# A decoder layer on one core: silu and two high-part copies of ScalarE put behind its next copy out of PSUM

## The chip, the cores and the metric

The kernel runs on one core of one Trainium2 chip. The metric is the device time of one execution in microseconds (us): 1008.36 us before the change, the median of 3 runs (1008.08 to 1009.29). In the profile the engines are called PE (TensorE, matmuls), PEld (TensorE's weight loads), DVE (VectorE), ACT (ScalarE), POOL (GpSimd) and SP (SyncE, which issues most DMAs). Each engine works through its own list of instructions in order; an instruction that must wait for another engine holds up all that stand behind it in its list.

## The reference

One hybrid decoder layer in float32, SEQ = 256 tokens, D_MODEL = 2048: attention heads and pooling mixers behind one input projection, an output projection into the residual, and then a gated MLP of width D_FF = 5632. The change touches the MLP alone:

```python
def conv_ffn(h, w_up, conv_w, conv_b, w_down):
    u = h @ w_up                                   # 2048 -> 2 * 5632
    u_pad = jnp.pad(u, ((0, 0), (CONV_WIDTH - 1, 0), (0, 0)))
    y = conv_b
    for i in range(CONV_WIDTH):                    # causal, 3 taps
        y = y + conv_w[i] * u_pad[:, i:i + S]
    gate, val = jnp.split(y, 2, axis=-1)
    return (jax.nn.silu(gate) * val) @ w_down
```

## The kernel before, in words

**Numbers in two parts.** A float32 matrix is split into a high part (rounded by a copy to the type fp32r) and a low part (the matrix less its high part). ACT makes the high part with an `activation` copy, DVE the low part with a subtraction. A product is then three matmuls: high by high, high by low, low by high. Weights arrive in chunks of 128 x 2048 elements, 1 MB each: SP loads a chunk into `raw` (`load`), ACT writes `wh` (`high`, L182), DVE writes `wl` (`low`, L188), and that frees `raw` for a later load. In the part of the program looked at here ACT makes `wh` three chunks ahead of PE, and DVE `wl` two chunks ahead.

**The MLP in three thirds.** The 5632 hidden features are taken in groups of 256, and the groups in three thirds of 8, 8 and 6. A third first computes all its groups ("up": for each group a gate block and then a value block, `ps_feat`, L276 and L278), then multiplies its result `hid` by `w_down` ("down": `ps_down`, L876). A block is four halves of 8 pairs of matmuls, and two chunks of weights. In the down stage of five, five and three groups of a third the product of 2 x 2 quarters is done in seven products in place of eight. Those need sums of quarters of the activations (`left_sums`) and of the weights; the latter DVE makes from loaded quarters during the up stage (`make`, L196 to L198), one per pair of blocks in most pairs, and SP stores them.

**What follows a block.** When PE has finished a block, `conv_in` brings it out of PSUM: ACT copies one half of the columns into a scratch tile `fs` (L545, "the copy" below), DVE adds the other half (L546, "the add") and writes `u`, scaled by row (L799). At the start of the next block ACT forms the three taps of the convolution, `y` and two `z` (L809 and L811, six instructions). One chunk later DVE sums them (`taps`, L817, two instructions). For a gate block ACT then applies silu in place (L827). For a value block DVE multiplies by the gate (L843, "the product"), ACT writes the high part of `hid` (L844), and one chunk later DVE writes the low part (L856) and, for the groups with seven products, the sums `ls` (L865 to L867), whose high part ACT writes to `sums` (L869) and whose low part DVE writes one chunk later (L870).

**What sets the order.** The program is written out by hand, one step per half block. A step first issues what falls due at the start of a chunk (`wh`, `wl`, `make`, then what `later` put on an agenda for this step), then what is in `deferred`, then the matmuls, and after a block's last half `conv_in`. Thus in ACT's list silu of a gate block stands ahead of the copy of the following value block, and the high part of `hid` ahead of the copy of the following gate block. The scratch tiles `fs` and `z` share a ring of two buffers (`scratch`), so the copy of a block takes the buffer of the first `z` of the block before it.

Of the kernel before, what the change touches and what calls it, by code (L numbers as in the profile page):

```python
# [23 lines left out]
F32 = mybir.dt.float32  # L24
F32R = mybir.dt.float32r
AF = mybir.ActivationFunctionType
OP = mybir.AluOpType
# [69 lines left out]
def layer(ctx: ExitStack, tc: tile.TileContext, xT, wts, mix, mix12, par, rel_d, ident_d, icnt_d, out):  # L97
    nc = tc.nc
# [32 lines left out]
    late, turn_of = {}, [0]  # L131
# [411 lines left out]
    def add_halves(dst, ps):  # L543

        nc.scalar.activation(dst, ps[:, :, S:], AF.Copy)  # L545
        nc.vector.tensor_tensor(dst, ps[:, :, :S], dst, op=OP.add)  # L546

    def pool_window(ps, g):

        s = early.tile([P, 2, S], F32, name="pst", tag=("sq", "hn")[g % 2], bufs=(1, 3)[g % 2])  # L550
        add_halves(s, ps)
        nc.vector.tensor_tensor(pa[0][:, :, PAD:], s, rrow[:, None, :].to_broadcast([P, 2, S]), op=OP.mult)
        st["win", g] = s
# [45 lines left out]


    steps, hooks, pre, deferred = [], [], {}, []
    hold, splits, now, agenda = set(), [], [0], {}
    where = []

    def later(n, f):
        agenda.setdefault(now[0] + n, []).append(f)
# [106 lines left out]
    def block(name, dt=F32):  # L713
        return late["pool"].tile([P, SPAD + 1024], dt, name=name, tag="sums", bufs=5)[:, SOFF:SOFF + 1024]

    def residual(ps, g):
        x2, s = x2_tiles(2 * g, 2 * g + 2), scratch("fs")
        add_halves(s, ps)
        nc.vector.tensor_tensor(x2, s, x2, op=OP.add)
        if g == 0:  # L720
            nc.scalar.activation(late["sq"], x2, AF.Square)
            return
        s = late["pool"].tile([P, 2, S], F32, name="xs", tag="y0")
        nc.scalar.activation(s, x2, AF.Square)
        nc.vector.tensor_tensor(late["sq"], late["sq"], s, op=OP.add)
# [44 lines left out]
    def stats2():  # L770
        late["rrow"] = keep.tile([P, S], F32, name="rrow2", tag="rrow")
        a, b = scratch("rs0"), scratch("rs1")
        t = a[:, 0, :]
        mean_sq(t.rearrange("p (j a) -> p a j", a=32), late["row"].rearrange("p (a j) -> p a j", j=8))
        rsqrt(late["rrow"], t, S, late["pool"], (a[:, 1, :], b[:, 0, :]))
# [19 lines left out]
    def conv_in(ps):  # L795

        s = scratch("fs")
        add_halves(s, ps)
        nc.vector.tensor_tensor(late["u"][:, :, 2:], s, late["rrow"][:, None, :].to_broadcast([P, 2, S]), op=OP.mult)  # L799

    def conv(f0_, which):

        u = late["u"]
        y = late["pool"].tile([P, 2, S], F32, name="y", tag=f"y{which}")
        z = [scratch("z") for _ in range(2)]
        for m in range(2):
            f = f0_ + m
            cw = [col(C_CW + i * 2 * NF + f) for i in range(3)]
            nc.scalar.activation(y[:, m, :], u[:, m, 2:], AF.Identity, scale=cw[2], bias=col(C_CB + f))  # L809
            for i in range(2):  # L810
                nc.scalar.activation(z[i][:, m, :], u[:, m, 1 - i:1 - i + S], AF.Copy, scale=cw[1 - i])  # L811
        return y, z

    def taps(y, z):

        for t in z:
            nc.vector.tensor_tensor(y, y, t, op=OP.add)  # L817
        return y

    def gate(ps, g):  # L820
        if g == 0:
            stats2()
        conv_in(ps)

        def rest(parts):
            y = taps(*parts)
            nc.scalar.activation(y, y, AF.Silu)  # L827
            late["gate"] = y

        def start():  # L830
            parts = conv(2 * g, 0)
            later(2, lambda: rest(parts))
        deferred.append(start)

    def value(ps, g, j, seven, end):
        conv_in(ps)

        def rest(parts):
            if j == 0:
                late["hid"] = keep.tile([P, KT, 2, S], F32R, name="hid", tag="c")  # L840
            y = taps(*parts)
            hid, ks = late["hid"], slice(2 * j, 2 * j + 2)
            nc.vector.tensor_tensor(y, y, late["gate"], op=OP.mult)  # L843
            nc.scalar.activation(hid[:, ks, 0, :], y, AF.Copy)  # L844
            later(2, lambda: rest2(y, hid, ks))

        def start():
            parts = conv(NF + 2 * g, 1)
            if end:
                rest(parts)  # L850
            else:
                later(2, lambda: rest(parts))
        deferred.append(start)

        def rest2(y, hid, ks):
            nc.vector.tensor_tensor(hid[:, ks, 1, :], y, hid[:, ks, 0, :].bitcast(F32), op=OP.subtract)  # L856
            if seven:
                late["S", j] = left_sums(y)

    def left_sums(y):  # L860

        y = y.rearrange("p a (b n) -> p (a b) n", n=P)
        a11, a21, a12 = (y[:, i, :] for i in range(3))
        s = late["pool"].tile([P, 2, S], F32, name="ls", tag="ls").rearrange("p a (b n) -> p (a b) n", n=P)
        nc.vector.tensor_tensor(s[:, :2, :], y[:, 0:4:3, :], y[:, 1:2, :].to_broadcast([P, 2, P]), op=OP.subtract)  # L865
        nc.vector.tensor_tensor(s[:, 2, :], s[:, 1, :], a11, op=OP.add)
        nc.vector.tensor_tensor(s[:, 3, :], a12, s[:, 2, :], op=OP.subtract)  # L867
        parts = block("sums", F32R).rearrange("p (a b n) -> p a b n", a=2, n=P)
        nc.scalar.activation(parts[:, 0], s, AF.Copy)  # L869
        later(2, lambda: nc.vector.tensor_tensor(parts[:, 1], s, parts[:, 0].bitcast(F32), op=OP.subtract))  # L870
        return parts

    def product(ps, left, right, first, last):
# [241 lines left out]
```

## Time and profile before

| | before |
|---|---|
| time, median of 3 runs | 1008.36 us |
| the profiled execution: time, span | 1010.49 us, 1008.7 us |
| busy share of the span: PE, PEld, DVE, ACT | 99%, 85%, 81%, 60% |
| mean granted TensorE clock | 0.995 |
| MLP's first third: up, down | 177.33 us, 85.88 us |
| second third: up, down | 177.36 us, 87.44 us |
| last third: up, down | 130.60 us, 61.20 us |

The stages are cut where the matmuls change from `ps_feat` to `ps_down` and back. A row of a timeline has the start, the duration, the engine, the line and operation with the tiles written and read, and in brackets how long the engine was idle before it and what ended that. A row of waits has who waited for what, the total in us, how often, and the longest. A matmul's duration is modelled and overlaps the next; from the start of one matmul to the start of the next is the time that it holds the engine.

### The profile page before, as it was taken

Reading aid. Unit: us, or ns where it says so; the run is one execution under the profiler, and the core shown is the slowest. Engines: PE = TensorE matmul, PEld = TensorE weight load, DVE = VectorE, ACT = ScalarE, POOL = GpSimd, SP = SyncE. Lnnn points to the kernel's source line nnn. Section 1 sums busy time; section 2 is a strip of 40 time slices with the busy share of each in tenths; the row PEclk is TensorE's granted clock in tenths of the full one; section 3 lists DMA queues with packets and bytes.
Section 4 is the critical chain, followed back from the end, with each engine's and each line's share of the span. In section 5 each row is a group of like instructions: output and inputs, shape, how many; then the busy total and the mean of one; then the engine's idle time right before and its main releaser. Section 6 shows DMA issues by size and latency. Waiting matters only on the chain.

```text
span 1008.7 us, 13494 instructions
## 1 busy us (share of the span) xinstructions
PE 993.8 (99%) x5276; PEld 854.3 (85%) x5276; DVE 818.8 (81%) x853; ACT 608.6 (60%) x719; POOL 74.6 (7%) x134
## 2 busy tenths in 40 slices
PE   9999999999999999998999999999989999999998
PEld 7888888888888888886888888888868888888886
DVE  6776859866678878888989788888888888888896
ACT  6654545555548566666655556666774756666742
POOL 0202232211103300000000000000000000000000
PEclk9999999999999999999999999999989999999999
DMA  9958785699977887677977889777777988866682
GB/s 352 319 210 271 259 258 196 210 327 368 321 204 245 305 329 280 250 275 255 395 264 306 312 312 378 293 273 274 262 275 278 373 303 316 316 252 255 223 317 101
DMA packets 48895, 285.34 MB, mean 283 GB/s; under 512 B 6696, under 2 KB 9128, under 8 KB 20352
## 3 DMA queue, kind: packets, MB, share of 16 engines
q1 hardware_dynamic: 41776, 264.17, 70.6%
q0 software_dynamic: 7056, 20.33, 7.6%
q8 instruction: 41, 0.67, 0.3%
q14 instruction: 22, 0.18, 0.1%
HBM read 253.14 MB, written 39.72 MB: 290 GB/s over the span
## 4 chain that ended last, share of the span: by engine, by line
PE 61%; DVE 19%; issue 7%; ACT 7%; DMA 5%; POOL 1%; SPq 0%; DVEq 0%; ACTq 0%; POOLq 0%
PE ps_feat L276 22%; PE ps_down L876 20%; PE ps_feat L278 11%; DVE wl L188 8%; PE ps_val L254 4%; DVE y L817 2%; DVE fs L546 2%; ACT z L811 2%; PE ps_tok L264 2%; ACT fs L545 1%; ACT wh L182 1%; ACT y L809 1%; DVE raw L196 1%; DVE u L799 1%; DMA qT<-q1d 1%
## 5 line engine op out<-in xcount | busy, mean ns | idle before, releaser
L276 PE MATMUL ps_feat<-x2h,wh 128*128 128x512 f32 x1406 | 480.6, 390 | 0.0
L188 DVE TENSOR_TENSOR wl<-raw,wh 128x2048 fp32r<-128x2048 f32 (+1 forms) x171 | 376.0, 2204 | 25.2 <-PE ps_down L876 8.6
L278 PE MATMUL ps_feat<-x2h,wl 128*128 128x256 f32 x1408 | 390.2, 277 | 2.1 <-DVE wl L188 1.7
L182 ACT ACTIVATE wh<-raw 128x2048 fp32r<-128x2048 f32 (+1 forms) x171 | 316.0, 1852 | 101.2 <-PE ps_down L876 66.4
L276 PEld LDWEIGHTS ps_feat<-x2h,wh 128*128 128x128 f32 x1406 | 263.8, 188 | 55.6
L278 PEld LDWEIGHTS ps_feat<-x2h,wl 128*128 128x128 f32 x1408 | 264.2, 188 | 5.1 <-DVE wl L188 5.0
L876 PE MATMUL ps_down<-wh,hid 128*128 128x512 f32 x444 | 143.2, 391 | 0.0
L160 DVE TENSOR_TENSOR wl<-raw,wh 128x2048 fp32r<-128x2048 f32 (+3 forms) x44 | 83.0, 1894 | 37.7 <-ACT wh L159 29.2
L546 DVE TENSOR_TENSOR fs<-ps_feat,fs 128x512 f32<-128x512 f32 x52 | 36.0, 692 | 83.8 <-ACT fs L545 83.8
L876 PEld LDWEIGHTS ps_down<-wh,hid 128*128 128x128 f32 x444 | 84.1, 189 | 17.6
L876 PE MATMUL ps_down<-wl,hid 128*128 128x512 f32 x222 | 87.3, 393 | 0.8 <-DVE wl L188 0.8
L276 PE MATMUL ps_feat<-cat,wh 128*128 128x512 f32 x256 | 87.3, 389 | 0.0
L264 PE MATMUL ps_tok<-wh,xh 128*128 128x512 f32 x256 | 80.0, 391 | 0.0
L811 ACT ACTIVATE z<-u,pv 128x256 f32<-128x256 f32 x176 | 79.2, 499 | 0.0
L159 ACT ACTIVATE wh<-raw 128x2048 fp32r<-128x2048 f32 (+3 forms) x44 | 69.3, 1598 | 10.5 <-DMA raw<-in_wts 7.3
L876 PE MATMUL ps_down<-wh,sums 128*128 128x512 f32 x208 | 71.3, 400 | 0.0
L278 PE MATMUL ps_feat<-cat,wl 128*128 128x256 f32 x256 | 70.7, 276 | 0.0
L817 DVE TENSOR_TENSOR y<-y,z 128x512 f32<-128x512 f32 x88 | 60.7, 690 | 8.7 <-ACT z L811 2.7
L844 ACT ACTIVATE hid<-y 128x512 fp32r<-128x512 f32 x22 | 13.9, 633 | 81.8 <-DVE y L843 81.8
L264 PEld LDWEIGHTS ps_tok<-wh,xh 128*128 128x128 f32 x256 | 48.1, 188 | 10.0
L276 PEld LDWEIGHTS ps_feat<-cat,wh 128*128 128x128 f32 x256 | 48.1, 188 | 10.0
L809 ACT ACTIVATE y<-u,pv 128x256 f32<-128x256 f32 x88 | 51.9, 590 | 0.0
(189 smaller groups left out, 1033.2 us busy)
## 6 DMA issues: line engine op xcount, KB each, us to landing
raw<-in_wts SPq DMA_DIRECT2D x152, 1024.0 KB, 7.0
raw<-mixed SPq DMA_DIRECT2D x26, 1024.0 KB, 6.7
raw<-in_mix SPq DMA_DIRECT2D x22, 1024.0 KB, 6.3
mixed<-raw SPq DMA_DIRECT2D x22, 1024.0 KB, 5.2
raw<-in_wts SPq DMA_DIRECT2D x26, 768.0 KB, 5.1
raw<-in_wts SPq DMA_DIRECT2D x4, 512.0 KB, 6.8
mixed<-in_mix POOLq DMA_DIRECT2D x4, 512.0 KB, 13.7
mixed<-mixed POOLq DMA_DIRECT2D x8, 256.0 KB, 8.6
```

The lines of the kernel that those rows point to most:

```text
L159: nc.scalar.activation(wh, w, AF.Copy)
L160: nc.vector.tensor_tensor(wl, w, wh.bitcast(F32), op=OP.subtract)
L182: nc.scalar.activation(w, raws[c][:, :width(c)], AF.Copy)
L188: nc.vector.tensor_tensor(wl, raws[c][:, :width(c)], wh.bitcast(F32), op=OP.subtract)
L264: nc.tensor.matmul(ps[:, t, :], act[:, k0 + k, a, ts], w[:, ws], start=(first and k == 0 and n == 0), stop=(last and k == 1 and n == 2))
L276: nc.tensor.matmul(ps, wh[:, ws], act[:, k, :, :], start=(bool(first) and n == 0), stop=False, skip_group_check=True)
L278: nc.tensor.matmul(ps[:, S:], wl[:, ws], act[:, k, 0, :], start=False, stop=(last and n == len(ks) - 1), skip_group_check=True)
L546: nc.vector.tensor_tensor(dst, ps[:, :, :S], dst, op=OP.add)
L809: nc.scalar.activation(y[:, m, :], u[:, m, 2:], AF.Identity, scale=cw[2], bias=col(C_CB + f))
L811: nc.scalar.activation(z[i][:, m, :], u[:, m, 1 - i:1 - i + S], AF.Copy, scale=cw[1 - i])
L817: nc.vector.tensor_tensor(y, y, t, op=OP.add)
L876: nc.tensor.matmul(ps, a, w, start=(first and n == 0), stop=(last and n == 2), skip_group_check=True)
```

## The change

Three instructions of ACT are no longer issued where they are written but put into a list, `pending`: silu of the gate, the high part of `hid` and the high part of `sums`. `add_halves` issues all of the list right behind its copy. For the last value block of a third the high part of `hid` is still issued at once. The low part of `sums` on DVE is due four half blocks after the sums were formed, in place of two.

```diff
     def add_halves(dst, ps):
         nc.scalar.activation(dst, ps[:, :, S:], AF.Copy)
+        while pending:
+            pending.pop(0)()
         nc.vector.tensor_tensor(dst, ps[:, :, :S], dst, op=OP.add)
...
         def rest(parts):
-            y = taps(*parts)
-            nc.scalar.activation(y, y, AF.Silu)
-            late["gate"] = y
+            y = late["gate"] = taps(*parts)
+            pending.append(lambda: nc.scalar.activation(y, y, AF.Silu))
...
             nc.vector.tensor_tensor(y, y, late["gate"], op=OP.mult)
-            nc.scalar.activation(hid[:, ks, 0, :], y, AF.Copy)
+            pending.append(lambda: nc.scalar.activation(hid[:, ks, 0, :], y, AF.Copy))
+            if end:
+                pending.pop()()
             later(2, lambda: rest2(y, hid, ks))
...
-        nc.scalar.activation(parts[:, 0], s, AF.Copy)
-        later(2, lambda: nc.vector.tensor_tensor(parts[:, 1], s, parts[:, 0].bitcast(F32), op=OP.subtract))
+        pending.append(lambda: nc.scalar.activation(parts[:, 0], s, AF.Copy))
+        later(4, lambda: nc.vector.tensor_tensor(parts[:, 1], s, parts[:, 0].bitcast(F32), op=OP.subtract))
```

ACT's list in the middle of the first third, from the copy of a gate block to the chunk behind the copy of the following value block. The lines of the changed file are 2 or 3 higher: L809, L811, L827, L844 and L869 before are L811, L813, L829, L845 and L872. Before:

```order
L844 ACTIVATE hid<-y 128x2x256
L545 ACTIVATE fs<-ps_feat 128x512
L182 ACTIVATE wh<-raw 128x2048
L869 ACTIVATE sums<-ls 128x512
L809 ACTIVATE y<-u,pv 128x256
L811 ACTIVATE z<-u,pv 128x256 x2
L809 ACTIVATE y<-u,pv 128x256
L811 ACTIVATE z<-u,pv 128x256 x2
L182 ACTIVATE wh<-raw 128x2048
L827 ACTIVATE y<-y 128x512
L545 ACTIVATE fs<-ps_feat 128x512
L182 ACTIVATE wh<-raw 128x2048
```

And in the changed kernel:

```order
L545 ACTIVATE fs<-ps_feat 128x512
L845 ACTIVATE hid<-y 128x2x256
L182 ACTIVATE wh<-raw 128x2048
L811 ACTIVATE y<-u,pv 128x256
L813 ACTIVATE z<-u,pv 128x256 x2
L811 ACTIVATE y<-u,pv 128x256
L813 ACTIVATE z<-u,pv 128x256 x2
L182 ACTIVATE wh<-raw 128x2048
L545 ACTIVATE fs<-ps_feat 128x512
L872 ACTIVATE sums<-ls 128x512
L829 ACTIVATE y<-y 128x512
L182 ACTIVATE wh<-raw 128x2048
```

Both copies now stand ahead of `hid` and of silu, and `sums` stands behind the second copy, no longer ahead of the taps `y` and `z`.

DVE's list at the same place, from the sums `ls` on. Before:

```order
L867 TENSOR_TENSOR ls<-y,ls 128x128
L188 TENSOR_TENSOR wl<-raw,wh 128x2048
L870 TENSOR_TENSOR sums<-ls,sums 128x512
L817 TENSOR_TENSOR y<-y,z 128x512 x2
L546 TENSOR_TENSOR fs<-ps_feat,fs 128x512
L799 TENSOR_TENSOR u<-fs,rrow_2598 128x2x256
L188 TENSOR_TENSOR wl<-raw,wh 128x2048
L196 TENSOR_TENSOR raw<-raw 128x1024
L197 TENSOR_TENSOR raw<-raw 128x512
L198 TENSOR_TENSOR raw<-raw 128x512
```

And in the changed kernel:

```order
L870 TENSOR_TENSOR ls<-y,ls 128x128
L188 TENSOR_TENSOR wl<-raw,wh 128x2048
L819 TENSOR_TENSOR y<-y,z 128x512 x2
L548 TENSOR_TENSOR fs<-ps_feat,fs 128x512
L801 TENSOR_TENSOR u<-fs,rrow_2598 128x2x256
L188 TENSOR_TENSOR wl<-raw,wh 128x2048
L196 TENSOR_TENSOR raw<-raw 128x1024
L197 TENSOR_TENSOR raw<-raw 128x512
L198 TENSOR_TENSOR raw<-raw 128x512
L873 TENSOR_TENSOR sums<-ls,sums 128x512
```

The low part of `sums` has moved behind the next add and the `make` that follows it; nothing else of DVE's list has moved. The lists of PE, SP and POOL are the same in both kernels.

ACT's list at the end of the first third, where the last value block is copied and the down stage begins. Before:

```order
L182 ACTIVATE wh<-raw 128x1536
L827 ACTIVATE y<-y 128x512
L545 ACTIVATE fs<-ps_feat 128x512
L182 ACTIVATE wh<-raw 128x2048
L809 ACTIVATE y<-u,pv 128x256
```

And in the changed kernel:

```order
L182 ACTIVATE wh<-raw 128x1536
L545 ACTIVATE fs<-ps_feat 128x512
L829 ACTIVATE y<-y 128x512
L182 ACTIVATE wh<-raw 128x2048
L811 ACTIVATE y<-u,pv 128x256
```

Here silu stands between the copy and the last taps.

More of the change, by code (lines that the diff above doesn't have):

```diff
@@ L601, in layer @@
     steps, hooks, pre, deferred = [], [], {}, []
-    hold, splits, now, agenda = set(), [], [0], {}
+    hold, splits, now, agenda, pending = set(), [], [0], {}, []
     where = []
```

## The prediction

> **What bounds the kernel now.** I read the share of busy time first, to see which engine could be the bound.
>
> ```profile
> PE 993.8 (99%) x5276; PEld 854.3 (85%) x5276; DVE 818.8 (81%) x853; ACT 608.6 (60%) x719; POOL 74.6 (7%) x134
> ```
>
> Taken at its word, PE leaves 1008.7 - 993.8 = 14.9 us to gain at most. But modelled ends overlap, so I count matmuls by stage instead, in the view by windows, with the six stages of the MLP as windows. Its columns are the stretch, its length, busy time and instructions of PE, PEld, DVE, ACT and POOL, the granted clock, the DMA share and GB/s.
>
> ```profile
> 284.69:462.02 177.33, 175.90 (x1026) 154.16 (x1025) 149.48 (x162) 116.90 (x160) 20.78 (x38) 1.00 0.77 274
> 462.02:547.90 85.88, 82.68 (x357) 67.40 (x356) 74.89 (x56) 53.62 (x41) 0.00 (x0) 0.98 0.82 313
> 547.90:725.26 177.36, 176.66 (x1027) 154.46 (x1025) 150.06 (x154) 112.79 (x152) 0.00 (x0) 1.00 0.79 298
> 725.26:812.70 87.44, 83.90 (x356) 68.29 (x355) 74.83 (x56) 53.98 (x42) 0.00 (x0) 0.96 0.81 303
> 812.70:943.30 130.60, 130.60 (x770) 115.90 (x769) 110.82 (x110) 85.27 (x114) 0.00 (x0) 1.00 0.76 285
> 943.30:1004.50 61.20, 61.20 (x272) 50.50 (x270) 51.56 (x43) 31.46 (x26) 0.00 (x0) 1.00 0.57 212
> ```
>
> The last third runs without a gap: 12 blocks in 130.60 us are 10.883 us each, and its 270 down matmuls in 61.20 us are 0.2267 us each. At that pace the 16 blocks of the other thirds would take 174.13 us, and their 354 down matmuls (two column halves of five groups with 21 and three with 24) 80.24 us. So PE loses 3.20, 5.64, 3.23 and 7.20 us there: **19.27 us in all**, part as gaps, part as matmuls at a lower clock (0.98 and 0.96). [...]
>
> Who does PE wait for, and who does that engine wait for? These are rows of the views of waits of PE and of DVE.
>
> ```profile
> PE ps_down L876 <- DVE wl L188: 6.7, 4, 3.0
> PE ps_feat L278 <- DVE wl L188: 1.7, 5, 0.6
> ...
> DVE fs L546 <- ACT fs L545: 83.8, 52, 3.8
> ```
>
> PE waits for DVE's low parts, and DVE's largest wait is its add, for ACT's copy. Is that a wait for PE's block behind the copy, and so harmless? The view of the tile `fs`, for ACT in the up stage of the second third, says no:
>
> ```profile
> L545 ACT ACTIVATE fs<-ps_feat x15: 575/580/600, 559.0 to 721.9; 128x512 f32<-128x512 f32 x15
> ...
>   PE ps_feat L278: 3.6, 1
> ```
>
> Only the first of 15 copies waits for PE. They come (721.9 - 559.0) / 14 = 11.64 us apart, where PE needs 10.883: DVE and ACT fall behind by 0.75 us a block until PE has used up its two chunks of low parts. Here is one pair of blocks of that regime, DVE's timeline and then ACT's.
>
> ```profile
> 664.60 0.69 DVE L546 TENSOR_TENSOR fs<-ps_feat,fs 128x512 f32<-128x512 f32 x1 [1.72 <-ACT fs L545]
> ...
> 672.93 1.48 DVE L817 TENSOR_TENSOR y<-y,z 128x512 f32<-128x512 f32 x2
> 674.44 0.69 DVE L843 TENSOR_TENSOR y<-y 128x512 f32<-128x512 f32 x1
> 676.38 0.69 DVE L546 TENSOR_TENSOR fs<-ps_feat,fs 128x512 f32<-128x512 f32 x1 [1.24 <-ACT fs L545]
> ...
> 683.71 0.68 DVE L870 TENSOR_TENSOR sums<-ls,sums 128x512 fp32r<-128x512 f32 x1
> 684.48 1.49 DVE L817 TENSOR_TENSOR y<-y,z 128x512 f32<-128x512 f32 x2
> 687.69 0.69 DVE L546 TENSOR_TENSOR fs<-ps_feat,fs 128x512 f32<-128x512 f32 x1 [1.73 <-ACT fs L545]
> ```
>
> ```profile
> 675.23 0.63 ACT L844 ACTIVATE hid<-y 128x512 fp32r<-128x512 f32 x1 [4.46 <-DVE y L843]
> 675.77 0.58 ACT L545 ACTIVATE fs<-ps_feat 128x512 f32<-128x512 f32 x1
> 676.25 1.91 ACT L182 ACTIVATE wh<-raw 128x2048 fp32r<-128x2048 f32 x1
> 681.62 0.63 ACT L869 ACTIVATE sums<-ls 128x512 fp32r<-128x512 f32 x1 [3.47 <-DVE ls L867]
> 682.16 0.59 ACT L809 ACTIVATE y<-u,pv 128x256 f32<-128x256 f32 x1
> ...
> 684.75 1.92 ACT L182 ACTIVATE wh<-raw 128x2048 fp32r<-128x2048 f32 x1
> 686.56 0.62 ACT L827 ACTIVATE y<-y 128x512 f32<-128x512 f32 x1
> 687.08 0.58 ACT L545 ACTIVATE fs<-ps_feat 128x512 f32<-128x512 f32 x1
> ```
>
> This is a circle. DVE's product ends at 675.13; only then can `hid` start (675.23), behind it the copy, and DVE, with nothing left ahead of its add, waits 1.24 us. In the other half the late `sums` (it waited for `ls`) pushes taps, `wh`, silu and copy back, and DVE waits 1.73 us. The pair takes 687.69 - 664.60 = 23.09 us, of which DVE works 23.09 - 2.97 = 20.12 us. PE needs 2 x 10.883 = 21.77 us. Without these waits DVE would be faster than PE by 1.65 us a pair.
>
> **The change part by part.** *Copy ahead of `hid` and silu.* It no longer waits for the product or the last tap, but it still needs the buffer of the first `z`, so the first of the two tap sums. In the value half that one ends about 672.93 + 0.70 = 673.63 (half of the row of two); with the 0.10 us from product to `hid` the copy runs 673.73 to 674.31, before the product's end at 675.13. In the gate half: first sum done 685.18, copy 685.28 to 685.86, DVE free at 685.97. Both waits go to nothing: 2.97 us a pair, and DVE's pair becomes 20.12 us. If the copy had to wait for the second sum after all, it would end 0.7 us later, and the gate half would wait about 0.6 us: 20.7 us a pair, still under 21.77.
>
> *`hid` and silu behind the copy.* Between copy and `wh` now stand 0.54 us (675.23 to 675.77), 0.52 us (686.56 to 687.08) and for `sums` 0.54 us more (681.62 to 682.16). Behind them wait `wh` and the taps, and for the taps DVE. In the gate half, counted from DVE's add: `hid` starts at about 0.05, `wh` at 0.6, the taps 1.81 us later (684.75 to 686.56) at 2.4, done after 2.59 us (682.16 to 684.75) at 5.0. DVE arrives there after 684.48 - 676.38 = 8.10 us, less the 0.77 of the moved `sums` row, at 7.33: 2.3 us to spare. In the value half `sums` and silu stand there, but `sums` no longer delays the taps, and DVE arrives later still, since `make` is in this half. `wh` is needed by DVE a whole chunk later. Cost: nothing; if the cover of 2.3 us were gone, up to 0.54 + 0.52 + 0.54 = 1.6 us a pair.
>
> *Low part of `sums` four halves later.* The same 0.77 us, moved from the lighter half to the one with `make`. That half becomes (676.38 - 664.60) - 1.24 + 0.77 = 11.31 us and the other 11.31 - 1.73 - 0.77 = 8.81; the sum is the same, and the excess of 0.43 us over 10.883 is made good in the next half. `sums` itself is not read before the down stage. No DMA and no instruction is added or taken away.
>
> *What then sets the pace.* PE. The lag shrinks in place of growing, so the gaps of 3.20 and 3.23 us go. Left are the entries to the down stages. These rows are PE's first low-part matmul of `sums` in the first and the last third, and what leads there in the last: copy, taps, and the low part in question.
>
> ```profile
> 476.41 0.80 PE L876 MATMUL ps_down<-wl,sums 128*128 128x512 f32 x1 [2.98 <-DVE wl L188]
> 477.00 1.05 PE L876 MATMUL ps_down<-wh,sums 128*128 128x512 f32 x2
> ...
> 953.76 0.39 PE L876 MATMUL ps_down<-wl,sums 128*128 128x512 f32 x1
> ```
>
> ```profile
> 944.40 0.58 ACT L545 ACTIVATE fs<-ps_feat 128x512 f32<-128x512 f32 x1
> ...
> 949.00 1.49 DVE L817 TENSOR_TENSOR y<-y,z 128x512 f32<-128x512 f32 x2 [0.90 <-ACT z L811]
> 951.13 2.28 DVE L188 TENSOR_TENSOR wl<-raw,wh 128x2048 fp32r<-128x2048 f32 x1
> ```
>
> In the last third the copy starts 1.10 us behind the stage's end (943.30), the low part is ready 953.41 - 944.40 = 9.01 us later, and PE uses it at 953.76, 10.46 us into the stage: 0.35 us to spare. In the first third the copy is late, so PE waits 2.98 us, and the next matmuls are slow as well. After the change silu stands in this chain (the taps are what DVE waits for): 9.01 + 0.52 = 9.53 us. But a copy that waits only for PE starts at once:
>
> ```profile
> 558.82 0.39 PE L276 MATMUL ps_feat<-x2h,wh 128*128 128x512 f32 x1
> ...
> 559.02 0.60 ACT L545 ACTIVATE fs<-ps_feat 128x512 f32<-128x512 f32 x1 [3.63 <-PE ps_feat L278]
> ```
>
> The first row is the first matmul of the next block, so the copy starts 0.20 us behind the block's end. 0.20 + 9.53 = 9.73, against 10.46: 0.7 us to spare in all three thirds, if DVE has caught up by the last block. It has: without `make` that half is among the light ones. So the 5.64 and 7.20 us go too.
>
> On the slow matmuls: the pace after the 2.98 us wait is (477.86 - 477.00) / 2 = 0.43 us, twice 0.2267. [...] The trace decides: slow matmuls follow, and they go with the wait.
>
> **Sum.** 3.20 + 5.64 + 3.23 + 7.20 = 19.27 us off the span of 1008.7, which gives 989.4. The profiled execution took 1010.49 us, 1.8 us around its span, and stands 2.1 us over the median of the runs; against the median the sum gives 1008.36 - 19.27 = 989.1. I add 0.5 us for what is left of the lag where the work is thickest (two `make` a pair early in the second third): **989.6 us**.
>
> **The rivals.**
>
> *A. The entries stay.* The up stages lose nothing any more, but the chain through silu and the taps still makes the first down low parts late. For: only 0.7 us to spare, and the chain grew by 0.52 us. Against: the last third passes even with a lag of 1.10 us. Price: if all of it stays, 1008.4 - 6.4 = 1001.9 us; with half of it, 995.5.
>
> *B. The wait changes its name.* DVE waits as long as before at another place, for `z`, for `sums`, or for the weights' transfer, so its pair stays over 21.77 us. For transfers speaks this row of ACT's waits, against it the small total over 14 times:
>
> ```profile
> ACT wh L182 <- DMA raw<-in_wts: 19.1, 14, 4.0
> ```
>
> It needs over 1.65 us a pair of new waiting to matter and 2.97 to undo all: 1008 us.
>
> *C. Slower.* The moved instructions make ACT's taps late for DVE: in every pair the two sums of taps wait on top of what DVE waits now. It decides from the point where the 2.3 us of cover are gone and new waits pass 2.97 us. Price: 1.06 us (silu and `sums`) for each of the last three pairs of two thirds, where PE already waits, so 6.4 us: 1015 us. Against it: ACT works 0.54 + 0.54 + 0.52 + 2 x 0.48 + 4 x 1.81 + 2 x 2.59 = 15.0 us of a pair of 21.77.
>
> **How the numbers follow.** The forecast gets 0.83, A 0.11 (half or more of the entries left), B 0.04, C 0.02. The forecast's own range is 988 to 992. To leave out no more than 2 in 10 the range must reach into A, to its case with half of the entries left and some more: **988 to 997 us**. A measurement of this kernel can tell about 0.2% (2 us) from no change: faster 0.94 (forecast and A), within 0.2% 0.04, slower 0.02.
>
> **What would show it.** In the changed profile the add's wait for the copy should stay, but with the copies waiting for PE, and 10.9 us apart in all thirds; the up stages of the first two thirds should last about 174.1 us and the down stages 80.3, with a granted clock of 1.00; PE's wait for low parts in `ps_down` should be gone. A shows in down stages over 82 us; B in copies 11.5 us apart with DVE waiting for something else; C in DVE's waits at L819 for `z`. I would be wrong if the copy still stood behind the product, or if PE's own pace fell.

## The result, and the profile after

The changed kernel takes **991.51 us**, the median of 4 runs (991.43 to 992.03), against 1008.22 us (1006.65 to 1009.29, 4 runs): a ratio of 0.9837, 95% interval 0.982 to 0.9854, so 16.7 us faster. The forecast was 989.6 us, the range 988 to 997 us.

The profiled execution took 992.03 us with a span of 990.3. This is the view by windows for the six stages of the MLP, cut as before (length, busy time and instructions of PE, PEld, DVE, ACT and POOL, granted clock, DMA share, GB/s):

```profile
285.52:459.60 174.08, 174.08 (x1026) 153.95 (x1025) 153.17 (x166) 120.19 (x163) 20.88 (x38) 1.00 0.80 293
459.60:539.87 80.27, 80.27 (x357) 66.45 (x355) 70.05 (x51) 50.95 (x37) 0.00 (x0) 1.00 0.81 310
539.87:713.99 174.12, 174.12 (x1026) 154.27 (x1025) 154.24 (x158) 116.59 (x156) 0.00 (x0) 1.00 0.83 314
713.99:794.26 80.27, 80.27 (x357) 66.45 (x356) 70.07 (x51) 50.98 (x37) 0.00 (x0) 1.00 0.80 307
794.26:924.86 130.60, 130.60 (x771) 115.76 (x769) 110.61 (x110) 85.58 (x114) 0.00 (x0) 1.00 0.76 291
924.86:986.06 61.20, 61.20 (x272) 50.49 (x270) 51.01 (x42) 31.64 (x26) 0.00 (x0) 1.00 0.53 199
```

All six stages run at PE's pace: the first four have become shorter by 3.25, 5.61, 3.24 and 7.17 us, the last two are the same to 0.01 us, and the granted clock is 1.00 everywhere. Together they take 700.54 us in place of 719.81, so 19.27 us less, the sum of the prediction.

The waits of PE, DVE and ACT, from the view of waits:

```profile
PE ps_val L245 <- ACT wh L159: 1.2, 2, 1.0
...
DVE fs L548 <- ACT fs L545: 62.7, 30, 5.9
...
ACT fs L545 <- PE ps_feat L278: 116.6, 37, 4.0
...
ACT wh L182 <- DMA raw<-in_wts: 34.2, 19, 6.8
...
ACT fs L545 <- DVE y L819: 13.1, 6, 3.8
```

PE's largest item is now 1.2 us in two waits, at the very start of the program; DVE no longer appears in its list for the MLP. DVE still waits 62.7 us for the copy, but 37 of the 52 copies now wait for PE (9 before, 26.2 us). The wait has the same name and has become harmless. Six copies wait for the first sum of taps (L819), whose `z` holds their buffer, as the prediction said they might.

### The profile page after: what moved, and what is told of

Same layout as the page of the kernel before. It is cut to its first block, busy times and chain, and to the rows that moved or that the text cites. A ratio compares the mean times of both kernels' runs of the same rounds, so it can differ in the third digit from the quotient of the medians.

```text
span 990.3 us, 13469 instructions
## 1 busy us (share of the span) xinstructions
PE 983.8 (99%) x5276; PEld 850.7 (86%) x5276; DVE 816.2 (82%) x853; ACT 610.4 (62%) x719; POOL 74.7 (8%) x134
## 4 chain that ended last, share of the span: by engine, by line
PE 91%; issue 4%; DMA 3%; DVE 1%; POOL 1%; SPq 0%; ACT 0%; POOLq 0%; DVEq 0%
PE ps_feat L276 41%; PE ps_down L879 22%; PE ps_feat L278 21%; PE ps_val L254 4%; PE ps_tok L264 2%; DMA qT<-q1d 1%; DMA eT<-e3d 1%; PE ps_pool L285 1%; DMA eT<-e0d 1%; DMA q0d<-q0x 1%; DMA raw<-in_wts 0%; DVE wl L160 0%; POOL qT L476 0%; DMA e0d<-e0x 0%; PE ps_s L497 0%
## 5 line engine op out<-in xcount | busy, mean ns | idle before, releaser
L545 ACT ACTIVATE fs<-ps_feat 128x512 f32<-128x512 f32 x52 | 31.0, 597 | 131.3 <-PE ps_feat L278 116.6
L548 DVE TENSOR_TENSOR fs<-ps_feat,fs 128x512 f32<-128x512 f32 x52 | 35.9, 689 | 63.0 <-ACT fs L545 62.7
L813 ACT ACTIVATE z<-u,pv 128x256 f32<-128x256 f32 x176 | 79.0, 497 | 0.0
L879 PE MATMUL ps_down<-wh,sums 128*128 128x512 f32 x208 | 69.2, 389 | 0.0
L819 DVE TENSOR_TENSOR y<-y,z 128x512 f32<-128x512 f32 x88 | 60.6, 689 | 9.2 <-ACT z L813 4.3
L811 ACT ACTIVATE y<-u,pv 128x256 f32<-128x256 f32 x88 | 51.7, 587 | 0.0
```

What stands on the lines that cost most here:

```text
L879: nc.tensor.matmul(ps, a, w, start=(first and n == 0), stop=(last and n == 2), skip_group_check=True)
```

## The experiments

**The kernel before, once more.** A second trace of it, to see how far the losses differ from one execution to the next.

> The kernel before once more, for a second trace. If the executions of it differ (1006.65 to 1009.29 us, 1010.49 in the profiled one) by how long TensorE's clock stays low behind the waits at the entries of the down stages, then the gaps in the up stages and the two waits of about 3 us are the same as in the first trace to 0.3 us, and only the slow matmuls behind them differ, by 1 to 3 us. If the waits themselves differ, the up stages or the rows of waits differ by that much.

It took 1009.95 us. Its first four stages by windows:

```profile
284.94:460.93 175.99, 175.19 (x1026) 154.01 (x1025) 149.09 (x162) 116.42 (x159) 20.75 (x38) 1.00 0.76 276
460.93:548.46 87.53, 83.97 (x357) 68.38 (x356) 75.35 (x56) 53.99 (x42) 0.00 (x0) 0.96 0.82 308
548.46:726.19 177.73, 177.17 (x1027) 154.81 (x1025) 150.44 (x154) 113.29 (x153) 0.00 (x0) 1.00 0.80 298
726.19:812.14 85.95, 82.75 (x357) 67.42 (x356) 74.87 (x56) 53.63 (x41) 0.00 (x0) 0.98 0.80 307
```

Against PE's pace they lose 1.9, 7.3, 3.6 and 5.7 us, 18.5 in all (3.2, 5.6, 3.2 and 7.2 in the first trace). The waits for low parts in `ps_down` are the same to the digit, 6.7 us in four; the slow matmuls behind them differ, 1.7 us more in one stage and 1.5 less in the other, as expected. But the gap of the first up stage differs too, by 1.3 us, which was not: there DVE and ACT enter the stage 1 us less late. So the losses are not a constant of the kernel; what the traces show of the slow matmuls behind equal waits stands below, at the doses.

**One part at a time.** Four kernels, each with some of the three moves. Is the gain shared out among the parts, or is it all there as soon as DVE's pair is no longer than PE's?

`hid` alone:

```diff
-            nc.scalar.activation(hid[:, ks, 0, :], y, AF.Copy)
+            pending.append(lambda: nc.scalar.activation(hid[:, ks, 0, :], y, AF.Copy))
+            if end:
+                pending.pop()()
```

> Only the high part of hid is put behind the copy; silu and sums stand where they stood before. Threshold theory (nothing is lost while DVE's pair of blocks is no longer than PE's 21.77 us): the value half loses its wait of 1.24 us, the pair takes 23.09 - 1.24 = 21.85 us, so DVE falls behind by only 0.04 us a block, and nearly all of the gain is there: up stages of the first two thirds within 0.3 us of 174.1, down stages 80.3 to 83 (the lag from the start of the first third no longer shrinks, so its entry may still wait), 992 to 996 us. Share theory (each part brings the share of the removed wait that it removes): 1.24 of 2.97 of the measured 16.7 us, so 7.0 us: 1001 us.

Silu alone:

```diff
-            y = taps(*parts)
-            nc.scalar.activation(y, y, AF.Silu)
-            late["gate"] = y
+            y = late["gate"] = taps(*parts)
+            pending.append(lambda: nc.scalar.activation(y, y, AF.Silu))
```

> Only silu is put behind the copy. Threshold theory: in the gate half the copy comes 0.52 us earlier (686.56 in place of 687.08), since sums still delays the taps; the pair takes 23.09 - 0.52 = 22.57 us, 0.80 over PE, against 1.32 over it before. The lag grows by 0.40 us a block and just reaches PE's two chunks at the end of a third: gaps in the up stages of 0 to 1 us each, entries to the down stages nearly as before, 1001 to 1004 us. Share theory: 0.52 of 2.97 of 16.7 us, 2.9 us: 1005 us.

`sums` alone:

```diff
-        nc.scalar.activation(parts[:, 0], s, AF.Copy)
-        later(2, lambda: nc.vector.tensor_tensor(parts[:, 1], s, parts[:, 0].bitcast(F32), op=OP.subtract))
+        pending.append(lambda: nc.scalar.activation(parts[:, 0], s, AF.Copy))
+        later(4, lambda: nc.vector.tensor_tensor(parts[:, 1], s, parts[:, 0].bitcast(F32), op=OP.subtract))
```

> Only the high part of sums is put behind the copy, its low part two halves later. Threshold theory: taps and wh no longer wait for ls, silu starts right behind DVE's taps, and the copy ends 0.54 + 0.58 + 0.13 us after them: wait 1.22 in place of 1.73 us, with 1.24 us left in the value half. The pair takes 22.58 us: like silu alone, 1001 to 1004 us. Share theory: 0.51 of 2.97 of 16.7 us: 1005 us.

`hid` and silu, both edits above together:

> hid and silu are put behind the copy, sums stays ahead of the taps. Threshold theory: no wait in the value half, 1.20 us in the gate half (the copy ends at 687.14 in place of 687.66, DVE is free at 685.97); the pair takes 21.3 us, 0.4 less than PE needs. All of the gain is there, 991 to 993 us, though DVE still waits for the copy behind sums. Share theory: 1.76 of 2.97 of 16.7 us, 9.9 us: 998 us.

Measured, against 1009.72 us of the kernel before on the same chip:

| moved | time, median of 4 | ratio, 95% interval | DVE's pair (expected) |
|---|---|---|---|
| `hid` | 991.39 us | 0.9818 (0.9803 to 0.9832) | 21.76 (21.85) us |
| silu | 1000.74 us | 0.9914 (0.9887 to 0.994) | 22.58 (22.57) us |
| `sums` | 1002.64 us | 0.9931 (0.9914 to 0.9948) | 22.38 (22.58) us |
| `hid` and silu | 992.0 us | 0.9827 (0.981 to 0.9845) | 21.25 (21.3) us |

The pair is read from DVE's timeline in the second third's up stage, from one gate block's add to the next one's, always two rows on. `hid` alone:

```profile
640.58 0.69 DVE L548 TENSOR_TENSOR fs<-ps_feat,fs 128x512 f32<-128x512 f32 x1
651.88 0.69 DVE L548 TENSOR_TENSOR fs<-ps_feat,fs 128x512 f32<-128x512 f32 x1 [1.73 <-ACT fs L545]
662.34 0.68 DVE L548 TENSOR_TENSOR fs<-ps_feat,fs 128x512 f32<-128x512 f32 x1
```

Silu alone:

```profile
646.15 0.69 DVE L548 TENSOR_TENSOR fs<-ps_feat,fs 128x512 f32<-128x512 f32 x1 [1.24 <-ACT fs L545]
656.94 0.69 DVE L548 TENSOR_TENSOR fs<-ps_feat,fs 128x512 f32<-128x512 f32 x1 [1.20 <-ACT fs L545]
668.73 0.69 DVE L548 TENSOR_TENSOR fs<-ps_feat,fs 128x512 f32<-128x512 f32 x1 [1.25 <-ACT fs L545]
```

`hid` and silu:

```profile
641.50 0.69 DVE L548 TENSOR_TENSOR fs<-ps_feat,fs 128x512 f32<-128x512 f32 x1
652.30 0.69 DVE L548 TENSOR_TENSOR fs<-ps_feat,fs 128x512 f32<-128x512 f32 x1 [1.20 <-ACT fs L545]
662.75 0.68 DVE L548 TENSOR_TENSOR fs<-ps_feat,fs 128x512 f32<-128x512 f32 x1
```

With `hid` moved the value half (second row to third) starts its add without a wait, and the gate half keeps its 1.73 us; with silu moved it is the gate half that falls to 1.20 us and the value half that keeps 1.24. That is the circle taken apart, wait by wait. The time follows the threshold and not the share: `hid` alone removes 1.24 of 2.97 us, the share theory gave it 1001 us, and it takes 991.39 us, all of the gain, because its pair of 21.76 us is no longer than the 21.77 us that PE needs. The other 1.73 us then cost nothing, and silu and `sums` on top of `hid` bring no time that these runs could tell (991.39, 992.0 and 991.51 us). Silu or `sums` alone leave the pair above PE's, and their loss is now mostly at the entries: in `sums` alone the second third reads

```profile
544.67:720.35 175.68, 175.38 (x1027) 154.59 (x1025) 150.71 (x155) 114.10 (x154) 0.00 (x0) 1.00 0.81 302
720.35:803.97 83.62, 80.64 (x356) 66.31 (x355) 73.91 (x55) 52.80 (x40) 0.00 (x0) 1.00 0.82 314
```

with 1.5 us lost in the up stage and 3.4 in the down stage. Silu alone came out a little better than expected (1000.74 against 1001 to 1004): its entries lose 1.9 and 3.9 us, where I had expected nearly the 5.6 and 7.2 of before. Its trace is that of its fastest run, 998.58 us; the slowest took 1004.8.

**How much room the entry has, and what a wait there costs.** The prediction gave the chain from the last copy to the second group's low part 0.7 us to spare. In the changed kernel it stands so at the first third's end (the copy, the taps and the low part, and PE's use of it):

```profile
459.81 0.60 ACT L545 ACTIVATE fs<-ps_feat 128x512 f32<-128x512 f32 x1 [3.55 <-PE ps_feat L278]
...
464.94 1.49 DVE L819 TENSOR_TENSOR y<-y,z 128x512 f32<-128x512 f32 x2 [1.42 <-ACT z L813]
467.08 2.29 DVE L188 TENSOR_TENSOR wl<-raw,wh 128x2048 fp32r<-128x2048 f32 x1
...
470.06 0.39 PE L879 MATMUL ps_down<-wl,sums 128*128 128x512 f32 x1
```

The low part is ready at 467.08 + 2.29 = 469.37, PE uses it at 470.06: 0.69 us. To show that this chain decides, ScalarE writes the first tap of the last value block of each third again, 4, 6 or 8 times:

```diff
+            for _ in range(1 + again * (m == 0)):
-            nc.scalar.activation(y[:, m, :], u[:, m, 2:], AF.Identity, scale=cw[2], bias=col(C_CB + f))
+                nc.scalar.activation(y[:, m, :], u[:, m, 2:], AF.Identity, scale=cw[2], bias=col(C_CB + f))
...
-            parts = conv(NF + 2 * g, 1)
+            parts = conv(NF + 2 * g, 1, 4 if end else 0)
```

> The changed kernel, in which ScalarE writes the first tap of the last value block of each third four times more (the same values), 4 x 0.49 = 1.96 us in the chain from the copy to the low part of the second group's weights, which has 0.69 us to spare. Chain theory: PE waits 1.96 - 0.69 = 1.27 us at the entry of each down stage, in all three thirds; without a lower clock the down stages take 81.5, 81.5 and 62.5 us, and the time is 995.3 us. If the clock falls already behind such a wait, each stage takes 1.8 to 3.2 us more. If the chain were not what decides there, nothing changes: 991.5 us.

> The same with six more: 2.94 us, so a wait of 2.25 us in each third; without a lower clock 82.5, 82.5 and 63.5 us and 998.3 us in all; with it 1.8 to 3.2 us more in each stage. If the chain were not what decides, 991.5 us.

> The same with eight more: 3.92 us, so a wait of 3.23 us in each third, about what the kernel before waits in two of them. Without a lower clock 83.5, 83.5 and 64.4 us and 1001.2 us in all; with the slow matmuls that followed such waits there, 1.8 to 3.2 us more in each stage, 1006.6 to 1010.8 us.

They took 997.9, 1006.65 and 1011.44 us, one run each. PE's wait at the first entry, one row from each kernel's timeline (four, six, eight):

```profile
471.71 0.50 PE L880 MATMUL ps_down<-wl,sums 128*128 128x512 f32 x1 [1.73 <-DVE wl L188]
```

```profile
473.13 0.50 PE L880 MATMUL ps_down<-wl,sums 128*128 128x512 f32 x1 [3.00 <-DVE wl L188]
```

```profile
473.44 0.80 PE L880 MATMUL ps_down<-wl,sums 128*128 128x512 f32 x1 [4.27 <-DVE wl L188]
```

The waits are longer than the expected 1.27, 2.25 and 3.23 us, since a repeated write to the same tile costs more than I put it at. ACT's timeline with four:

```profile
462.39 3.13 ACT L812 ACTIVATE y<-u,pv 128x256 f32<-128x256 f32 x5
465.42 0.89 ACT L814 ACTIVATE z<-u,pv 128x256 f32<-128x256 f32 x2
```

From 462.39 to 465.42 are 3.03 us; less the 0.49 of the first one, (3.03 - 0.49) / 4 = 0.635 us for each repeat, in place of 0.49. So the doses were 2.54, 3.81 and 5.08 us; less 0.69 they give 1.85, 3.12 and 4.39, each 0.12 us more than the wait in the row. Every microsecond of the dose beyond the room is a wait of PE, in all three thirds: the chain decides, and 0.69 us was its room.

What follows the wait is in the first down stage of the three kernels, by windows:

```profile
459.37:541.66 82.29, 80.56 (x357) 66.37 (x355) 69.91 (x51) 53.23 (x41) 0.00 (x0) 1.00 0.78 301
```

```profile
459.52:544.71 85.19, 82.19 (x357) 67.53 (x355) 70.24 (x51) 54.54 (x43) 0.00 (x0) 0.98 0.77 293
```

```profile
458.55:546.15 87.60, 83.33 (x356) 68.41 (x355) 70.25 (x51) 55.75 (x45) 0.00 (x0) 0.96 0.74 282
```

Against 80.27 us they lose 2.0, 4.9 and 7.3 us for waits of 1.73, 3.00 and 4.27: 0.3 us beside the wait in the first, 1.9 and 3.1 in the others, whose granted clock is below 1.00. The length of the wait alone does not decide this. In `sums` alone PE waits 2.95 us at the first entry and 2.98 us at the second; slow matmuls follow the first and none the second, which loses 0.4 us beside its wait. The granted clock in the traces shows where the two differ. In the first trace of before it is one half from 476.28 to 479.69 us and from 739.10 to 745.93, so for 3.41 us behind the first entry and 6.83 us behind the second, and full for the 259.41 us between them, 76 times 3.41. These are slices of 3.41 us of that trace, two around the first entry and three around the second (length, PE's busy time, and further on the granted clock):

```profile
472.86:476.28 3.42, 0.57 (x3) 0.15 (x1) 3.39 (x4) 2.03 (x3) 0.00 (x0) 1.00 0.64 268
476.28:479.69 3.41, 3.28 (x8) 2.60 (x9) 3.41 (x4) 3.15 (x2) 0.00 (x0) 0.50 0.69 215
...
735.69:739.10 3.41, 1.38 (x6) 0.77 (x5) 3.27 (x4) 1.47 (x3) 0.00 (x0) 1.00 0.81 300
739.10:742.52 3.42, 2.50 (x6) 2.02 (x7) 3.42 (x4) 3.42 (x3) 0.00 (x0) 0.50 0.44 119
742.52:745.93 3.41, 3.41 (x9) 2.64 (x9) 3.10 (x2) 1.33 (x2) 0.00 (x0) 0.50 0.97 352
```

In `sums` alone the clock falls at 473.08 us. These are its slices of 3.41 us, counted from there, two around the first entry and three around the second:

```profile
469.66:473.08 3.42, 0.54 (x3) 0.11 (x1) 3.39 (x4) 2.09 (x3) 0.00 (x0) 1.00 0.63 266
473.08:476.49 3.41, 3.34 (x8) 2.67 (x9) 3.41 (x4) 3.09 (x2) 0.00 (x0) 0.50 0.71 223
...
729.08:732.49 3.41, 1.97 (x9) 1.29 (x7) 2.80 (x4) 1.47 (x5) 0.00 (x0) 1.00 0.76 267
732.49:735.90 3.41, 1.87 (x8) 1.58 (x9) 3.41 (x3) 3.41 (x4) 0.00 (x0) 1.00 0.39 99
735.90:739.30 3.40, 3.40 (x17) 2.82 (x16) 3.40 (x3) 3.36 (x3) 0.00 (x0) 1.00 0.92 345
```

The first wait lies in one slice and leaves PE idle for 2.88 us of it, and the next slice runs at half the clock. The second is cut in two, 1.44 and 1.54 us, and nothing follows. In the twelve traces the granted clock is below 1.00 in eleven down stages: two in each trace of before, the first of `sums` alone, and all three with six and with eight more writes, each behind a wait of about 3 us or more. It is 1.00 behind the waits of 1.73 and 1.74 us with four more writes, behind one of 2.8 us (silu alone, second third) and behind that of 2.98 us in `sums` alone. In the slices above, what followed a wait of about 3 us went with how much of it lay in one slice: 2.88 of 2.95 us (`sums` alone, first entry) and 2.03 of 2.95 us (before, second entry) were followed by half the clock, 1.54 of 2.98 us (`sums` alone, second entry) was not.

**Spending the room.** PE is now the bound, so fewer matmuls should be time saved. A fourth group of the last third is done in seven products, with two more `make`:

```diff
-SEVEN = ((1, 2, 3, 4, 5), (1, 2, 3, 4, 5), (1, 2, 3))
+SEVEN = ((1, 2, 3, 4, 5), (1, 2, 3, 4, 5), (1, 2, 3, 4))
...
-BY_DVE = ((2, 3, 4, 5, 6, 7), (0, 0.5, 1, 1.5, 2, 3, 4, 5, 6, 7), (0, 0.5, 1, 2, 3, 4))
+BY_DVE = ((2, 3, 4, 5, 6, 7), (0, 0.5, 1, 1.5, 2, 3, 4, 5, 6, 7), (0, 0.5, 1, 1.5, 2, 2.5, 3, 4))
```

> The changed kernel with a fourth group of the last third in seven products: 2 x 3 x 0.2267 = 1.36 us less for PE, two more make of 2.6 us, one more set of sums (1.75 us) for DVE and 4 MB more in transfers in the last third's up stage. Threshold theory: DVE's pairs there stay under 21.77 us, but for those with two make, whose lag the next ones make good; the down stage takes 59.8 us, the time 990.1 us. If the transfers or DVE's lag reach the entry, its stage loses 1 to 5 us: 991 to 995 us.

> The changed kernel again beside it, on the same chip: 991.5 us, within 1 us, and executions that differ by less than 1 us, since no wait at an entry is left whose clock could vary.

It took 994.93 us (993.39 to 995.59, 4 runs), the changed kernel beside it 991.75 us (five runs, four from 991.45 to 992.13 and one at 996.6, so more scatter than the 1 us that I had expected; that one has no trace, its granted clock was 1.0, and its cause stays open): 3.2 us slower by the medians. The last up stage stays at 130.6 us, but the down stage behind it takes 62.5 us, where 59.8 was expected, and the program ends 6.5 us after the start of its last matmul, where the changed kernel ends 4.4 us after it. These are rows of the view by windows (15 us of that stage) and of the view of waits from there to the end:

```profile
940.00:955.00 15.00, 14.83 (x66) 12.03 (x65) 12.19 (x10) 9.55 (x7) 0.00 (x0) 1.00 1.00 393
```

```profile
ACT wh L182 <- DMA raw<-mixed: 5.0, 2, 4.4
...
PE ps_down L879 <- DVE wl L188: 1.1, 2, 0.6
```

In these 15 us the transfers are at a share of 1.00 and 393 GB/s; later in the stage, from 967.3 to 971.7 us, ACT waits 4.4 us for the mixed weights, and PE for low parts behind them. The time is that of the second branch of the expectation, but the loss comes inside the stage and behind it, not at its entry. That the transfers are what makes it late is read from this trace; no run here varies them.

## Why the prediction was right, and where its numbers were off

**What bounds the kernel: right.** Counting matmuls per stage gave 19.27 us of loss, and the six stages became shorter by 19.27 us. PE's busy time gave 14.9. The weight loads' share, 85% of the span before, is 82 to 89% in the six stages at PE's pace (from 50.49 of 61.20 us to 115.76 of 130.60).

**The circle, and both waits going to nothing: right, and shown.** Where DVE is behind, its pair takes less than PE's: in the changed kernel

```profile
629.95 0.69 DVE L548 TENSOR_TENSOR fs<-ps_feat,fs 128x512 f32<-128x512 f32 x1
641.00 0.68 DVE L548 TENSOR_TENSOR fs<-ps_feat,fs 128x512 f32<-128x512 f32 x1
649.74 0.69 DVE L548 TENSOR_TENSOR fs<-ps_feat,fs 128x512 f32<-128x512 f32 x1
```

are 19.79 us from gate add to gate add with no wait, where 20.12 was forecast. The first sum of taps, not the second, is what the copy waits for.

**The room at the entries: right.** 0.69 us, forecast 0.7. The sentence ahead of the rows was wrong in the name: the matmuls at 476.41 and 953.76 are the first low-part products of the second group with `sums`, not of the first; the times were those of the right instruction. Rival A needed that room to be gone, and the doses show what it would have cost.

**Rival B's mechanism was there, below its threshold.** Early in the second third, with two `make` a pair, ACT waits for weights:

```profile
577.71 1.93 ACT L182 ACTIVATE wh<-raw 128x2048 fp32r<-128x2048 f32 x1 [3.81 <-DMA raw<-in_wts]
...
585.15 1.93 ACT L182 ACTIVATE wh<-raw 128x2048 fp32r<-128x2048 f32 x1 [2.93 <-DMA raw<-in_wts]
...
591.20 1.93 ACT L182 ACTIVATE wh<-raw 128x2048 fp32r<-128x2048 f32 x1 [3.12 <-DMA raw<-in_wts]
```

The lag rises to about 4 us and is made good by the faster pairs above; the stage still takes 174.12 us. I added 0.5 us for this, and it cost nothing.

**The time: off by 1.9 us, in the sum's last step.** The loss was that of one execution (1010.49 us), and I took it off the median of others (1008.36). The 2.1 us between them I carried over as if they would remain, but the time of before varies with these losses: the second trace lost 18.5 us, and the kernel before ran from 1006.65 to 1011.36 us in all. Against its own execution the sum gives 1010.49 - 19.27 = 991.2 us, and the median came out at 991.51. The 0.5 us for the lag was one too many. The profiled execution took a little longer than the median, 992.03 us; its MLP began 0.83 us later than that of before (285.52 for 284.69), in a part of the program that the change leaves alone.

**Rival C had no place.** No wait for `z` came near DVE's 2.97 us: in the chain at the entry it is 1.42 us, and that lies inside the room.

**The slow matmuls: they went with the waits, as predicted.** The granted clock is 1.00 in all six stages of the changed kernel. Where PE waits, waits of nearly the same length had different effects: the clock fell behind those of 2.98 and 2.95 us in the first trace of before, and in `sums` alone, of two in one execution, 2.95 and 2.98 us, only the first slowed what came behind.

## What to carry to other kernels

On an engine that works its list in order, put the copy that frees the next step ahead of work that nobody needs soon; a wait on its slot in the list was paid here by the engines that stand behind: by DVE with 2.97 us a pair, by PE with 19.27 us in all. Compare the loop of each engine with the loop of the bound engine: what matters is which side of that threshold a loop lies on. Here the smallest move that crossed it brought all of the gain, and the rest brought room: 21.76, 21.25 and 19.79 us a pair against PE's 21.77. To forecast a time, take the losses off the execution in which they were counted.

## What the runs showed of the hardware that I had not expected

In the first trace of before, TensorE's granted clock fell to one half for 3.41 us behind the first entry and for 6.83 us behind the second, with 259.41 us at the full clock between them. A slice of 3.41 us with 2.03 us of idle time (before, second entry) was followed by half the clock, a wait of 1.74 us (four more writes, second entry) was not. And the same wait had different prices: stages with a wait of 2.95 to 3.00 us lost between 0.4 us (`sums` alone, second third) and 3.7 us (the second trace of before, first third) beside their waits. At half the clock a matmul took 0.43 us in place of 0.227 (before, from 477.00 to 477.86 us for two). The half clock lasted one slice behind the first entry of before, where PE was idle for 0.13 us of that slice, and two behind the second, where it was idle for 0.92 us of the first of them. In the second trace it is the other way round, by the granted clock of the two stages: 0.96 and 0.98, where the first has 0.98 and 0.96. That is the 1.7 us more and 1.5 us less between them. And a repeated ACTIVATE into the same 128x256 half of a tile took 0.635 us from start to start (four more writes), where one followed by another tile's took 0.49.
